# A two-layer hybrid trunk: rows summed on TensorE between the layers and at the end, packed query columns, and constant matmuls ahead of estimated waits

## The chip, the cores and the metric

The kernel runs on one core of a Trainium2 chip. Time is device time in microseconds (us) from start to end of one execution. A core has TensorE (PE in the profile; PEld is its weight load), VectorE (DVE), ScalarE (ACT), GpSimd (POOL) and SyncE (SP), which run their own instruction streams and wait for each other by semaphores; matmuls write to PSUM, here eight banks of 128x512 float32. TensorE's clock has two levels, 2.4 and 1.2 GHz; the profile shows the level that was granted (PEclk, 1.00 or 0.50).

## The reference

256 latent rows `x` and 256 context rows of 1024 channels go through two layers; only the 256 latent rows are the output. A layer is

```python
h = rms_norm(x, norm1_g) * (1.0 + sc1) + sh1            # and hc from the context rows
... = split_in(h @ w_in)                                # for Hyena, gated DeltaNet (GDN), latent attention (MLA)
q = (rms_norm(cq, mla_q_norm_g) @ mla_w_uq)             # 8 heads of 64 plain + 32 rotary columns
qr_l = rope_2d(qr_l, row, col)                          # rotates the 32 columns in four groups of 8
mix = merge_branches(gate_l, y_hy, y_gdn, y_mla, w_out)
x = x + gt1 * mix
h2 = rms_norm(x, norm2_g) * (1.0 + sc2) + sh2
x = x + gt2 * moe_ffn(h2, ...)                          # top 2 of 16 experts, weighted by the gate
```

and the end is `rms_norm(x, final_norm_g)`. Layer 0 carries the context rows too (512 rows in all); layer 1 updates the latent rows alone.

## The kernel before

All matmuls are float32 in effect. Weights and activations of the mixers are split into two rounded halves each, and `mm3` (line 420) multiplies three of the four pairs; some smaller products are plain float32 matmuls, each of which the chip runs as two instructions. SBUF is an arena of 47 pages of 128x1024 float32 (`Arena`, line 145); every buffer named `pg` in the profile is a page or half page of it. PSUM banks are handed out in the order in which they came back (`bank`, `unbank`, lines 391 and 395).

The order of the work is not written by hand throughout. `Plan` (line 227) keeps an estimated clock for each engine and for each buffer; every instruction passes through a `Lane` (line 197), which enters it in the plan and then issues it. Weighted products are *items* (`Item`, line 336: loads, preparation, matmuls, a step after them) in one list for each layer (`layer`, line 2331), and long chains of small steps (GDN, Hyena, attention, routing) are *streams*, generators from which `tick` and `fill` take a step wherever the plan sees time. So a change of one piece can move others. Since each instruction is issued by `Lane`, almost all rows of the profile show its line, L210; they are told apart by engine, tile and time.

Stages: layer 0's mixers run to about 881 us, its experts to 1165, the step between the layers to 1199, layer 1's mixers to 1776, its experts to 2046, the end to 2079.

The pieces that the change touches:

- **Query projection** (`uq_item`, line 1600). One item for each head: its 96 columns are loaded, `swap` (line 863) copies the 32 rotary columns, exchanged in groups of eight, into columns 96 to 128, and 18 matmuls (6 blocks of 128 rows, three pairs) give the head's queries and their exchanged copy. Then ScalarE copies the plain 64 rows out of PSUM, and VectorE forms the rotation as two products and a sum. `abkr_item` (line 838) does the same for the key's rotary columns.
- **Experts.** Layer 0 takes the 16 experts one after the other. Layer 1 (`moe_sets`, line 2208) has 12 sets of four slots of 32 tokens, each slot with its expert: up products, activation, down products; then ScalarE and VectorE copy a set's 128x1024 result out of two banks, and GpSimd scatters its rows to the DRAM buffer `yd`, two rows for each token.
- **The overflow test** (`overflow`, line 2492). Every engine loads the largest expert count and jumps over the handling (line 2497) if no expert has more tokens than fit.
- **The sum** (`load_y`, line 2286, and `combine`, line 2295). The rows are loaded back from `yd`; for each tile of 128 tokens ScalarE scales the first row by its gate, VectorE adds the second times its gate, GpSimd multiplies by `gt2`, VectorE adds to `x`, ScalarE sums the squares. Between the layers that is four tiles; at the end two tiles in half rows, followed by the final RMS norm, in which GpSimd multiplies by the final gain.
- **Between the layers** the new rows are normalised (`norm_rows`) and transposed on TensorE against the identity (`cst`), for layer 1's projection.

Of the kernel before, what the change touches and what calls it, by code (L numbers as in the profile page):

```python
# [42 lines left out]
def _constants():  # L43
# [27 lines left out]
    ra, rb = np.zeros((128, SEQ)), np.zeros((128, SEQ))  # L71
    ra[32:64], ra[64:96] = c32, s32
    rb[64:96], rb[96:128] = c32, s32
    cols["ropeA"], cols["ropeB"] = ra, rb
# [122 lines left out]
class Lane:  # L197


    def __init__(self, plan, eng, name):  # L200
        self._plan, self._eng, self._name = plan, eng, name

    def __getattr__(self, op):
        f = getattr(self._eng, op)
        if not callable(f):
            return f

        def call(*a, **k):
# [3 lines left out]
        return call  # L212

# [13 lines left out]
class Plan:  # L227
# [5 lines left out]
    def __init__(self):  # L233
# [4 lines left out]
        self.warm = 0.0  # L238
# [12 lines left out]
    def when(self, ap):  # L251
        return max(self.done.get(k, 0.0) for k in self.keys(ap))

# [108 lines left out]
LAG = (2, 1)  # L362


class Trunk:
# [209 lines left out]
    def setup(self):  # L575
# [7 lines left out]
        self.yd = [self.dr.tile([1024 >> l, D], F32, name=f"yd{l}") for l in range(L)]  # L583
        self.tokd = [self.dr.tile([512 * NE, 1], I32, name=f"tokd{l}") for l in range(L)]
# [253 lines left out]
    def abkr_item(self, l):  # L838
# [8 lines left out]
        def prep0(pg):  # L847
            self.swap(pg, 32, 64, 8)

        def post(b):  # L850
            ab, kr, t2 = self.M.get(), self.M.get(), self.M.get()
            nc.scalar.copy(ab.f()[0:16], b[0:16, :])
            ra = self.c("ropeA")
            nc.vector.tensor_tensor(kr.f()[64:96, :SEQ], b[32:64, :SEQ], ra[32:64], op=OP.mult)
            nc.vector.tensor_tensor(t2.f()[64:96, :SEQ], b[64:96, :SEQ], ra[64:96], op=OP.mult)
            nc.vector.tensor_tensor(kr.f()[64:96, :SEQ], kr.f()[64:96, :SEQ], t2.f()[64:96, :SEQ], op=OP.add)
# [4 lines left out]
        return self.win(l, 0, 512, post, "abkr", loader, prep0)  # L861

    def swap(self, pg, a, b, k):

        src = pg[:, :, a:a + 32].rearrange("p k (u s c) -> p k u s c", u=2, s=2)
        dst = pg[:, :, b:b + 32].rearrange("p k (u s c) -> p k u s c", u=2, s=2)
        for u in range(2):
            for s in range(2):
                self.nc.vector.tensor_copy(dst[:, :, u, s, :], src[:, :, u, 1 - s, :])
# [730 lines left out]
    def uq_item(self, l, h):  # L1600

        nc, M = self.nc, self.M
        nt = 512 if l < L - 1 else 256
# [998 lines left out]
```

## Time and profile before

| quantity | value |
|---|---|
| times of three runs | 2080.86, 2086.78, 2089.03 us |
| median | 2086.78 us |
| the profiled execution: its time, its span | 2080.96 us, 2079.3 us |
| mean granted TensorE clock over the span | 0.940 |
| TensorE, VectorE busy | 1850.6 us (89%), 1300.7 us (63%) |
| ScalarE, GpSimd busy | 873.3 us (42%), 318.5 us (15%) |
| read from HBM | 391.94 MB, 200 GB/s over the span |

The share of an engine is an average over stages with different limits. A row of a timeline gives the start of a run of like instructions, its length, and in brackets how long the engine was idle before it and which engine or DMA ended that idle time. A float32 matmul counts as two instructions, so "x8" is four matmuls; a matmul of rounded halves is one instruction.

### The profile page before, as it was taken

How to read it: one execution, taken by the hardware profiler on the slowest of the kernel's cores; microseconds unless marked ns; L12 is line 12 of the kernel's file. 1: busy time of each engine (PE TensorE's matmuls, PEld its weight loads, DVE VectorE, ACT ScalarE, POOL GpSimd, SP SyncE). 2: the span in 40 equal slices, each digit the busy share in tenths (PEclk: the TensorE clock that was granted, in tenths of full speed). 3: DMA queues.
4: the chain of work that ended last, by engine and by line, in shares of the span. 5: the costliest groups of instructions: out<-in, count | busy, mean ns of one | idle time of the engine just before them, and what ended most of it. 6: DMA issues, size and time to landing. Idle time of an engine off the chain costs nothing. (4 is left out here: it accounts for less than half of the span.)

```text
span 2079.3 us, 32681 instructions
## 1 busy us (share of the span) xinstructions
PE 1850.6 (89%) x12412; PEld 1369.9 (66%) x12413; DVE 1300.7 (63%) x2799; ACT 873.3 (42%) x1520; POOL 318.5 (15%) x314
## 2 busy tenths in 40 slices
PE   4899998899999989699999488998989977899993
PEld 1776786677768777588888366787768966233331
DVE  2667566654675669799999676777777755111113
ACT  3342423444434534288888444443455432111111
POOL 2212112000032204311110201131011310100002
PEclk8999999999999999799999798999989988999997
DMA  9717212412253274689998585622415529799961
GB/s 334 256 62 218 70 38 57 111 42 82 92 182 80 85 247 162 243 326 386 380 381 314 152 282 170 174 55 57 120 31 163 143 86 391 248 394 391 385 256 70
DMA packets 295184, 401.10 MB, mean 193 GB/s; under 512 B 43892, under 2 KB 185722, under 8 KB 295016
## 3 DMA queue, kind: packets, MB, share of 16 engines
q1 hardware_dynamic: 271512, 360.38, 51.5%
q0 software_dynamic: 13056, 27.15, 3.7%
q10 hardware_dynamic: 10448, 11.37, 1.7%
q8 instruction: 100, 1.64, 0.3%
q14 instruction: 68, 0.56, 0.1%
HBM read 391.94 MB, written 23.20 MB: 200 GB/s over the span
## 5 line engine op out<-in xcount | busy, mean ns | idle before, releaser
L210 PE MATMUL bank<-pg,pg 128*128 128x512 f32 (+6 forms) x10746 | 1659.6, 390 | 57.8 <-ACT pg L210 31.3
L210 PEld LDWEIGHTS bank<-pg,pg 128*128 128x128 f32 (+4 forms) x10746 | 1212.8, 167 | 455.9 <-issue 203.9
L210 DVE TENSOR_TENSOR pg<-pg,pg 128x1024 fp32r<-128x1024 f32 (+11 forms) x699 | 608.5, 903 | 157.7 <-ACT pg L210 147.8
L210 ACT CAST pg<-pg 128x1024 fp32r<-128x1024 f32 (+3 forms) x460 | 428.8, 965 | 209.7 <-DVE pg L210 139.0
L210 ACT COPY pg<-bank 64x256 f32<-64x256 f32 (+5 forms) x402 | 163.7, 440 | 285.1 <-PE bank L210 238.0
L210 PE MATMUL bank<-cst,pg 128*128 128x128 f32 (+3 forms) x935 | 142.5, 290 | 103.7 <-DVE pg L210 64.1
L210 PEld LDWEIGHTS bank<-cst,pg 128*128 128x128 f32 (+1 forms) x935 | 118.2, 159 | 147.4 <-issue 51.6
L210 POOL TENSOR_TENSOR pg<-pg,pg 128x512 f32<-128x512 f32 (+3 forms) x72 | 119.6, 1667 | 441.2 <-DVE pg L210 196.2
L210 ACT ACTIVATE pg<-bank 128x512 f32<-128x512 f32 (+1 forms) x116 | 61.0, 535 | 166.9 <-PE bank L210 156.3
L210 ACT ACTIVATE pg<-pg 128x512 f32<-128x512 f32 (+4 forms) x77 | 52.7, 692 | 146.8 <-DVE pg L210 107.1
L210 DVE SCALAR_TENSOR_TENSOR pg<-bank,vec,pg 128x510 f32<-128x510 f32 (+3 forms) x112 | 73.5, 657 | 54.6 <-ACT pg L210 52.8
L210 DVE SCALAR_TENSOR_TENSOR pg<-pg,bank 128x512 f32<-128x512 f32 (+1 forms) x92 | 54.2, 602 | 77.2 <-ACT pg L210 64.7
L210 POOL DMA_INDIRECT yd<-pg,t_vi x28 | 29.0, 1037 | 465.3 <-ACT pg L210 235.8
L210 DVE TENSOR_TENSOR pg<-bank,pg 128x512 fp32r<-128x512 f32 (+4 forms) x120 | 69.1, 596 | 27.3 <-ACT pg L210 14.6
L210 ACT CAST pg<-bank 128x512 fp32r<-128x512 f32 (+1 forms) x72 | 35.6, 517 | 100.4 <-PE bank L210 80.2
L210 DVE TENSOR_TENSOR pg<-pg,bank 128x512 f32<-128x512 f32 (+1 forms) x44 | 27.0, 613 | 80.6 <-PE bank L210 77.8
L210 POOL TENSOR_TENSOR pg<-pg 128x512 f32<-128x512 f32 (+1 forms) x12 | 14.3, 1193 | 400.0 <-ACT pg L210 348.3
L210 ACT ACTIVATE pg<-bank,t_amx,t_asq 128x512 f32<-128x512 f32 (+1 forms) x48 | 34.0, 708 | 77.4 <-DVE t_amx L210 77.4
L210 ACT ACTIVATE pg<-bank,vec 128x512 f32<-128x512 f32 (+3 forms) x64 | 41.4, 647 | 59.5 <-PE bank L210 53.6
L210 DVE COPY pg<-bank 128x512 f32<-128x512 f32 x12 | 8.3, 692 | 82.2 <-PE bank L210 75.3
L210 PE MATMUL bank<-pg,sc 128*32 128x512 f32 x384 | 53.5, 630 | 0.8 <-DMA pg<-in_w_ada_dram 0.7
L210 DVE TENSOR_REDUCE pg<-pg 128x128 f32<-128x1024 f32 (+15 forms) x128 | 43.1, 337 | 4.4
(258 smaller groups left out, 814.0 us busy)
## 6 DMA issues: line engine op xcount, KB each, us to landing
pg<-in_moe_w_dram SPq DMA_DIRECT2D x384, 512.0 KB
pg<-in_w_in_dram SPq DMA_DIRECT2D x120, 512.0 KB
pg<-in_w_ada_dram SPq DMA_DIRECT2D x96, 512.0 KB
pg<-in_w_out_dram SPq DMA_DIRECT2D x24, 512.0 KB
pg<-yd SPq DMA_DIRECT2D x12, 512.0 KB
pg<-in_mla_w_uq_dram SPq DMA_DIRECT2D x16, 288.0 KB
pg<-gcd POOLq DMA_DIRECT2D x16, 256.0 KB, 4.1
pg<-in_hy_out_dram SPq DMA_DIRECT2D x8, 512.0 KB
```

The costliest lines, as they stand in the source:

```text
L210: return f(*a, **k)
```

## The change

1. *Query projection.* Eight items become six: `rotary` items take the 32 rotary columns of four heads, `plain` items the 64 plain columns of two heads. The exchanged copy is no longer multiplied: VectorE makes it from the result with `stream_shuffle` by the index list `TURN`. `swap` is gone, and the constants of the rotation become two tables of 128 rows.
2. *Between the layers.* `combine` weights tiles 1 and 3 on TensorE: two diagonal matrices for a tile (`diagonals`, made before the rows are there) times the two rows, summed in PSUM. VectorE multiplies all tiles by `gt2`, GpSimd none.
3. *The end.* Layer 1's last two sets are not scattered. `tail_weights`, started at the first expert product of set 3, prepares each slot's gate (`gws`) and one-hot matrices from slots to tokens (`hot`); after set 9's scatter a stream `partial` adds what sets 0 to 9 left in `yd` (whose rows are zeroed early in the layer by `zero_rows`); and `finish` adds the last two sets by eight matmuls with `hot`, then normalises and stores. The handling of overflow zeroes the rows and adds them again.
4. *Constant matmuls.* Ahead of a transpose, or of a matmul that starts a sum, `keep_busy` asks the plan how long TensorE would wait. Between 1.5 and 14 us by that estimate, it fills 0.6 of it with matmuls of the identity by itself into the place that the next instruction overwrites. That gives 133 such matmuls in 14 places.

```diff
+        if self._name == "tensor" and (op == "transpose" or k.get("start")):
+            self.keep_busy(op, a, k)
...
+    def keep_busy(self, op, a, k):
+        plan, o = self._plan, a[0]
+        w = math.prod(o.shape[1:])
+        gap = plan.begin("tensor", op, a, k) - plan.clk["tensor"]
+        if plan.off or self._filling or plan.idle is None or o.shape[0] != 128 or w < 64 or not 1500 < gap < 14000:
+            return
+        w = min(w, 128)
+        c = 2 * max(4 + 0.84 * 128, 38 + 0.835 * w)
+        self._filling = True
+        for _ in range(int(0.6 * gap / c)):
+            self.matmul(o[:, :w], plan.idle, plan.idle[:, :w], start=True, stop=True)
+        self._filling = False
...
+DIAG = (1, 3)
+TAIL = (NSET - 2, NSET - 1)
+TURN = [i ^ 8 for i in range(32)]
...
+        def rotary(it):
+            r, t = M.get(), M.get()
+            nc.scalar.copy(r.f(nt), it.b[:, :nt])
+            self.unbank(it.b)
+            x, y = t.f(SEQ), t.f(SEQ, SEQ)
+            v.stream_shuffle(y, r.f(SEQ), TURN)
+            v.tensor_tensor(x, r.f(SEQ), self.c("ropeC"), op=OP.mult)
+            v.tensor_tensor(y, y, self.c("ropeS"), op=OP.mult)
+            for j in range(4):
+                q = self.qt[4 * i + j] = M.get()
+                p = slice(32 * j, 32 * j + 32)
+                v.tensor_tensor(q.f(SEQ)[64:96], x[p], y[p], op=OP.add)
...
+                if n in TAIL:
+                    for hf, b in enumerate(st.pop((n, "y"))):
+                        nc.vector.scalar_tensor_tensor(y.f(512, 512 * hf), b, self.gws[:, n - TAIL[0]:n - TAIL[0] + 1], self.gt2[0].f(512, 512 * hf), op0=OP.mult, op1=OP.mult)
+                        self.unbank(b)
+                    self.tail[n] = y
+                    return
...
+                if n == TAIL[0] - 1:
+                    self.start("partial", self.partial(l))
...
+    def add_rows(self, l, t, eng):
+        nc, v = self.nc, self.nc.vector
+        src = self.yd[l][256 * t:256 * t + 256].rearrange("(p k) d -> p k d", k=2)
+        y0, y1 = self.M.get(2), self.M.get(2)
+        for i, y in enumerate((y0, y1)):
+            eng.dma_start(out=y.f(), in_=src[:, i, :])
+        yield self.plan.when(y1.f())
...
+    def finish(self, l):
...
+        for hf in range(2):
+            for j, n in enumerate(TAIL):
+                for t in range(2):
+                    if j == 0:
+                        bank[t] = self.bank()
+                    nc.tensor.matmul(bank[t], self.hot.f(128, 128 * (2 * j + t)), self.tail[n].f(512, 512 * hf), start=j == 0, stop=j == len(TAIL) - 1)
+            for t in range(2):
+                x = self.xt[t].f(512, 512 * hf)
+                v.tensor_tensor(x, x, bank[t], op=OP.add)
...
-    def combine(self, tiles, ys, parts, after):
+    def combine(self, ys, after):
...
+        for t in DIAG:
+            for hf in range(2):
+                b = bank[t, hf] = self.bank()
+                for i in range(2):
+                    nc.tensor.matmul(b, self.dg[t].f(128, 128 * i), ys[t, i].f(512, 512 * hf), start=i == 0, stop=i == 1)
...
-        items += [self.ukv_item(l)] + [self.uq_item(l, h) for h in range(8)]
+        items += [self.ukv_item(l)] + [self.uq_item(l, kind, i) for kind, i in (("rotary", 0), ("plain", 0), ("plain", 1), ("rotary", 1), ("plain", 2), ("plain", 3))]
```

Three places in TensorE's order. In its rows `bank` is the place in PSUM that is written, behind `<-` stand its two inputs, `cst` is the constants' buffer with the identity, and the numbers behind `pg` are the page and its use. The first place is TensorE in layer 0, ahead of the transposes of GDN that start at 759.38 us. Before:

```order
L210 MATMUL bank_67<-pg_81_421,pg_514_5780 128x512 x2
L210 MATMUL bank_67<-pg_81_421,pg_515_5781 128x512
L210 MATMUL bank_67<-pg_82_430,pg_514_5780 128x512 x2
L210 MATMUL bank_67<-pg_82_430,pg_515_5781 128x512
L210 MATMUL bank_64<-cst_71,pg_492_5374 128x128 x2
L210 MATMUL bank_64<-cst_71,pg_447_4766 128x128 x2
L210 MATMUL bank_68<-cst_71,pg_492_5374 128x128 x2
L210 MATMUL bank_68<-cst_71,pg_447_4766 128x128 x2
```

After:

```order
L210 MATMUL bank_64<-pg_83_422,pg_491_5290 128x512 x2
L210 MATMUL bank_64<-pg_83_422,pg_492_5291 128x512
L210 MATMUL bank_64<-pg_84_431,pg_491_5290 128x512 x2
L210 MATMUL bank_64<-pg_84_431,pg_492_5291 128x512
L210 MATMUL bank_63<-cst_71 128x128 x14
L210 MATMUL bank_63<-cst_71,pg_444_4718 128x128 x4
L210 MATMUL bank_69<-cst_71,pg_444_4718 128x128 x4
L210 MATMUL bank_66<-pg_298_3061,pg_517_5740 128x512 x2
```

The products of another stream stand ahead of the transposes in both; 14 constant matmuls now stand between, in the bank that the first transposes write.

The second is TensorE between the layers, from the jump of the overflow test to layer 1's first transposes. Before:

```order
L2511 UNCONDITIONAL_BRANCH x2
L2508 REGISTER_ALU
L2508 COMPARE_AND_BRANCH
L2508 UNCONDITIONAL_BRANCH
L2497 UNCONDITIONAL_BRANCH
L210 MATMUL bank_65<-cst_71,pg_1373_10008 128x128
L210 MATMUL bank_65<-cst_71,pg_1374_10010 128x128
L210 MATMUL bank_65<-cst_71,pg_1375_10012 128x128
L210 MATMUL bank_65<-cst_71,pg_1376_10014 128x128
```

After:

```order
L2628 UNCONDITIONAL_BRANCH
L2615 UNCONDITIONAL_BRANCH
L210 MATMUL bank_67<-pg_1343_9892,pg_1270_9538 128x512
L210 MATMUL bank_67<-pg_1344_9894,pg_1270_9538 128x512
L210 MATMUL bank_70<-pg_1343_9892,pg_1270_9538 128x512
L210 MATMUL bank_70<-pg_1344_9894,pg_1270_9538 128x512
L210 MATMUL bank_65<-pg_1347_9900,pg_1270_9538 128x512
L210 MATMUL bank_65<-pg_1348_9902,pg_1270_9538 128x512
L210 MATMUL bank_64<-pg_1347_9900,pg_1270_9538 128x512
L210 MATMUL bank_64<-pg_1348_9902,pg_1270_9538 128x512
L210 MATMUL bank_69<-cst_71 128x128 x21
L210 MATMUL bank_69<-cst_71,pg_1375_10005 128x128
```

Eight products with the diagonals and 21 constant matmuls now stand ahead of the first transpose.

The third is the end of TensorE's program. Before:

```order
L210 MATMUL bank_64<-pg_2100_17528,pg_2096_17507 128x512
L210 MATMUL bank_70<-pg_2100_17528,pg_2096_17507 128x512
L2511 UNCONDITIONAL_BRANCH x2
L2508 REGISTER_ALU
L2508 COMPARE_AND_BRANCH
L2508 UNCONDITIONAL_BRANCH
L2497 UNCONDITIONAL_BRANCH
```

After:

```order
L2628 COMPARE_AND_BRANCH
L2628 UNCONDITIONAL_BRANCH
L2615 UNCONDITIONAL_BRANCH x2
L210 MATMUL bank_68<-pg_2057_17283,pg_1870_15563 128x512
L210 MATMUL bank_66<-pg_2057_17283,pg_1870_15563 128x512
L210 MATMUL bank_68<-pg_2058_17318,pg_1870_15563 128x512
L210 MATMUL bank_66<-pg_2058_17318,pg_1870_15563 128x512
L210 MATMUL bank_70<-pg_2057_17283,pg_1870_15563 128x512
L210 MATMUL bank_69<-pg_2057_17283,pg_1870_15563 128x512
L210 MATMUL bank_70<-pg_2058_17318,pg_1870_15563 128x512
L210 MATMUL bank_69<-pg_2058_17318,pg_1870_15563 128x512
```

Where the program ended with the jump, eight matmuls with the one-hot page now follow; for each half the first of the two sets goes into both banks, then the second.

## Rows read from the trace of the kernel before

**Rows 1.** First part of the page: busy time, share, instructions of each engine.
```profile
PE 1850.6 (89%) x12412; PEld 1369.9 (66%) x12413; DVE 1300.7 (63%) x2799; ACT 873.3 (42%) x1520; POOL 318.5 (15%) x314
```

**Rows 2.** Timeline, end of the span: start, duration, engine, operation, [idle before, releaser].
```profile
2033.49 12.22 PE L210 MATMUL bank<-pg,pg 128*32 128x512 f32 x112
...
2045.79 0.69 DVE L210 COPY pg<-bank 128x512 f32<-128x512 f32 x1 [6.17 <-PE bank L210]
...
2068.68 2.22 DVE L210 TENSOR_SCALAR t_fss<-t_fss 128x2 f32<-128x2 f32 x1
...
2072.95 1.15 ACT L210 ACTIVATE pg<-pg,t_finb 128x1024 f32<-128x1024 f32 x1 [4.50 <-DVE t_finb L210]
...
2074.13 0.34 ACTq L210 DMA_DIRECT2D out_dram<-pg  x1
```

**Rows 3.** Timeline between the layers.
```profile
1177.37 1.28 DVE L210 SCALAR_TENSOR_TENSOR pg<-pg,t_gw,pg 128x1024 f32<-128x1024 f32 x1 [14.50 <-DMA pg<-yd]
...
1179.30 1.15 ACT L210 ACTIVATE pg<-pg,t_gw 128x1024 f32<-128x1024 f32 x1 [2.07 <-DMA pg<-yd]
...
1183.23 3.38 DVE L210 SCALAR_TENSOR_TENSOR pg<-pg,t_gw,pg 128x1024 f32<-128x1024 f32 x1
...
1198.85 1.04 PE L210 MATMUL bank<-cst,pg 128*128 128x128 f32 x3 [33.45 <-DVE pg L210]
```

**Rows 4.** Timeline of TensorE at three waits.
```profile
319.17 1.22 PE L210 MATMUL bank<-pg,pg 128*128 128x512 f32 x2 [7.02 <-ACT pg L210]
...
759.38 2.15 PE L210 MATMUL bank<-cst,pg 128*128 128x128 f32 x8 [4.86 <-DVE pg L210]
...
1702.06 1.11 PE L210 MATMUL bank<-cst,pg 128*128 128x128 f32 x4 [7.07 <-DVE pg L210]
```

**Rows 5.** Windows: us, busy of each engine (instructions), PEclk, DMA share, GB/s.
```profile
319.20:324.50 5.30, 4.92 (x11) 3.43 (x12) 5.09 (x12) 0.87 (x1) 2.00 (x2) 0.50 0.01 3
759.40:764.90 5.50, 5.50 (x17) 4.41 (x18) 3.33 (x5) 1.98 (x3) 0.00 (x0) 0.50 0.87 299
```

**Rows 6.** Timeline of TensorE; group by line and form: busy, mean ns.
```profile
36.10 1.98 PE L210 MATMUL bank<-pg,pg 64*128 64x512 f32 x4
...
48.93 3.78 PE L210 MATMUL bank<-pg,pg 64*128 64x512 f32 x4
...
L210 PE MATMUL bank<-pg,pg 128*128 128x128 f32 x724 | 100.0, 294 | 5.8 <-DVE pg L210 4.5 <-ACT pg L210 1.0
```

**Rows 7.** Timeline, set 9's scatter; DMA issues: count, KB each, us to landing.
```profile
2019.04 0.98 POOL L210 DMA_INDIRECT yd<-pg,t_vi  x1 [21.48 <-DVE pg L210]
...
pg<-xd POOLq DMA_DIRECT2D x2, 512.0 KB, 8.1
...
yd<-pg,t_vi POOLq DMA_INDIRECT x28, 6.9
```

**Rows 8.** Timeline of ScalarE's copies of query items; matmuls by form.
```profile
402.33 0.58 ACT L210 COPY pg<-bank 64x512 f32<-64x512 f32 x1
...
412.94 0.58 ACT L210 COPY pg<-bank 64x512 f32<-64x512 f32 x1
...
1425.09 0.37 ACT L210 COPY pg<-bank 64x256 f32<-64x256 f32 x1 [1.17 <-PE bank L210]
...
1459.32 0.37 ACT L210 COPY pg<-bank 64x256 f32<-64x256 f32 x1 [0.23 <-PE bank L210]
...
L210 PE MATMUL bank<-pg,pg 128*128 128x256 f32 x1872 | 253.0, 294 | 10.6 <-ACT pg L210 5.6 <-DVE pg L210 4.9
```

**Rows 9.** Line 2497, overflow test: min/median/max ns, first to last start us.
```profile
L2497 SPq EVENT_SEMAPHORE  x18: 17/17/17, 1136.6 to 2010.6; - x18
...
L2497 DVEq EVENT_SEMAPHORE  x4: 21/21/21, 1162.9 to 2046.8; - x4
...
L2497 SPq COMPARE_BRANCH  x2: 50/52/53, 1131.5 to 2004.3; - x2
L2497 DVEq COMPARE_BRANCH  x2: 63/68/72, 1162.3 to 2046.2; - x2
```

More of the change, by code (lines that the diff above doesn't have):

```diff
@@ L237, in __init__ @@
         self.cur, self.sin, self.off = None, False, False
-        self.warm = 0.0
+        self.warm, self.idle = 0.0, None
     @staticmethod
@@ L860, in post @@
             self.start("gates", self.gdn_gates(l, ab))
[L861 to L869, printed above, removed]
+        return self.win(l, 0, 512, post, "abkr", loader)
     def gdn_gates(self, l, ab):
@@ L1622, in mm @@
                 x.free()
-            if h == 7:
+            if kind == "plain" and i == 3:
                 for hi, lo in self.lora["q"]["x"]:
@@ new lines, in combine @@
+        ss, s8 = self.tiny(4, "css"), self.tiny(8, "css8")
+        bank = {}
+        for t in DIAG:
+            for hf in range(2):
+                b = bank[t, hf] = self.bank()
+                for i in range(2):
+                    nc.tensor.matmul(b, self.dg[t].f(128, 128 * i), ys[t, i].f(512, 512 * hf), start=i == 0, stop=i == 1)
+            self.dg[t].free()
+        for t in range(4):
+            g, x = self.gt2[t // 2], self.xt[t]
+            y0, y1 = ys[t, 0], ys[t, 1]
+            if t in DIAG:
+                for hf in range(2):
+                    o = 512 * hf
+                    v.tensor_tensor(y0.f(512, o), bank[t, hf], g.f(512, o), op=OP.mult)
+                    self.unbank(bank[t, hf])
+                    v.tensor_tensor(x.f(512, o), x.f(512, o), y0.f(512, o), op=OP.add)
+                    nc.scalar.activation(y1.f(512, o), x.f(512, o), AF.Square, accum_out=s8[:, 2 * t + hf:2 * t + hf + 1])
+            else:
+                nc.scalar.activation(y0.f(), y0.f(), AF.Copy, scale=self.gw[0][:, t:t + 1])
+                v.scalar_tensor_tensor(y0.f(), y1.f(), self.gw[1][:, t:t + 1], y0.f(), op0=OP.mult, op1=OP.add)
+                v.tensor_tensor(y0.f(), y0.f(), g.f(), op=OP.mult)
+                v.tensor_tensor(x.f(), x.f(), y0.f(), op=OP.add)
+                nc.scalar.activation(y1.f(), x.f(), AF.Square, accum_out=ss[:, t:t + 1])
+            y0.free()
+            y1.free()
+            after(t)
@@ L2331, in layer @@
+        for t in DIAG:
+            v.tensor_tensor(ss[:, t:t + 1], s8[:, 2 * t:2 * t + 1], s8[:, 2 * t + 1:2 * t + 2], op=OP.add)
+        return ss
     def layer(self, l):
@@ L2351, in layer @@
         items = [self.abkr_item(l)] + ([hook(self.late_setup)] if l == 0 else []) + qkv(0)
+        items += [hook(lambda: self.zero_rows(l, nc.gpsimd))] if l == L - 1 else []
         items += [self.dft_item(l)] + [self.z_item(l, h) for h in (0, 1)]
@@ L2453, in build @@
             else:
[L2454 to L2467 removed]
+                self.finish(l)
             for g in self.gt2:
@@ L2497, in overflow @@
         with tc.If(most > CAP[l]):
+            if l == L - 1:
+                self.zero_rows(l, nc.sync)
             blk = self.M.get()
@@ L2512, in overflow @@
                         self.overflow_part(l, e, j)
+            if l == L - 1:
+                for t in range(2):
+                    for _ in self.add_rows(l, t, nc.sync):
+                        pass
         self.plan.off = False
```

168 lines of the change are left out of this document (95 added, 73 removed).

## The prediction

> **What bounds the kernel now.** I read the page's first part first: TensorE is busy for 1850.6 of 2079.3 us, and no other engine passes 63% [rows 1]. So most of the span is TensorE's own work, and a matmul taken out of a saturated stretch is worth its whole duration. Then I looked for stretches in which TensorE does nothing. Two are long. One stands at the end: the last matmul ends 33.6 us before the span does [rows 2]. The other lies between the layers: TensorE starts at 1198.85 after 33.45 us without work [rows 3]. The remaining waits are short, but after them the granted clock stands at its lower level, 1.2 instead of 2.4 GHz, for some microseconds of full work [rows 4, 5]. The change touches all of these, so I price it by place, against the profiled execution of 2080.96 us (span 2079.3 us). That execution lies at the lower end of the runs shown; their median is 2086.78.
>
> **Part 1, the end.** Before, the last matmul ends at 2033.49 + 12.22 = 2045.71 and the span ends 33.6 us later, at 2079.3 [rows 1, 2]. In between lie the copies out of PSUM, a scatter to DRAM, the load back, the weighted sum of 256 rows, the RMS norm and the store. After, the last two sets never go to DRAM. Their product is weighted on VectorE, multiplied by one-hot matrices and added to a stream that already holds sets 0 to 9. I rebuild the chain from 2045.71:
> - The second half is weighted as long as the copy there takes, 0.69 us, until 2046.5; the first half is done about 0.9 us earlier, since its matmuls end first. The first one-hot matmul writes the bank that this first half frees (the order rows show the same bank number), so it starts at about 2046.1.
> - Eight float32 matmuls of 512 columns: two such (four instructions, since float32 runs as two) took 1.98 us at the full clock, so 0.99 each, 7.9 us, until 2054.0. At the lower clock two took 3.78, so 1.89 each [rows 6]; TensorE has been working until 2045.71, so I take the full clock.
> - The last addition takes 0.7 us (as the copy of a half row) and the product with the final gain about 1.3, until 2056.0; the squares on ScalarE run beside it.
> - The norm's small steps: from 2068.68 to 2072.95 they took 4.27 us, of which one, run beside GpSimd's product, took 2.22 [rows 2]. GpSimd does nothing here after the change, so I take 2.4 us, until 2058.4.
> - The scaling, 1.15 us on ScalarE as before and about 1.3 on VectorE, until 2059.7; then the store, 2079.3 - 2074.13 = 5.2 us [rows 2], until 2064.9.
>
> That is 14.4 us less. What hides the rest: the sum over sets 0 to 9 moves ahead of the last two sets' end. Set 9's scatter is issued at 2019.04; a scatter lands in 6.9 us in the median and a 512 KB load from GpSimd's queue takes up to 8.1 [rows 7], so four loads issued behind it land by about 2038, and two rounds of ScalarE and VectorE (about 4 us each) end by 2046. VectorE does them before it weights sets 10 and 11, so this cover is thin: it is behind by as much as the loads are late. The loads wait on GpSimd's queue, behind which nothing else is queued then. The ends for this part are 17 (norm steps and adds closer than I laid them) and 8 us. I take 14.
>
> **Part 2, the query projection.** Eight items of 18 matmuls per layer become six, since four heads' rotary columns now fill one item and the swapped copy of them is no longer multiplied but shuffled on VectorE. In layer 0 TensorE sets the pace there: the items' copies follow each other from 402.33 to 412.94 in three steps, 3.54 us each [rows 8]. Two items less: 7.1 us. In layer 1 the copies go from 1425.09 to 1459.32 in seven steps, 4.9 us each, with other work in between; the matmuls alone cost 18 x 253.0/1872 = 2.4 us an item [rows 8]. So between 4.9 and 9.8 us for two; I take 5, nearest to the matmuls' own time. The swaps on VectorE go too, and what replaces them is shorter; I price this at nothing, since the items' pace has it already. The new loads come in shorter runs; they are issued ahead of their use, so nothing again, and up to 2 us if that lead is gone.
>
> **Part 3, between the layers.** Before, four tiles go through ScalarE, VectorE, GpSimd and VectorE. One multiply-add on VectorE took 3.38 us there, beside GpSimd's product, as against 1.28 alone [rows 3]. After, GpSimd is out of it; tiles 0 and 2 cost VectorE three passes of about 1.25 us each, tiles 1 and 3 four of 0.69 each, 13 us in all from 1177.4 on, so 1190.5 if nothing waits. But tile 1 waits for four float32 matmuls which can start only when its rows are there (1179.30 for the first, by ScalarE's wait on the same kind of load), and TensorE has then been idle for 14 us: at 1.89 each two of them end at 1183.1 and four at 1186.9. Tile 2's scaling stands behind tile 1's squares on ScalarE, in order. This pushes the last square to about 1197, about 1 us later than before, with ends of 4 more and 3 less (if the clock rises within the first four).
>
> **Part 4, the filler.** At 14 places, 133 matmuls of 128 columns by constants stand ahead of a matmul of which the planner thinks that it waits. One such float32 instruction costs 100.0/724 = 0.138 us and so a matmul 0.276 [rows 6]; 21 of them stand in the idle stretch between the layers, the other 112 are 31 us of work. Where the wait is real they cost nothing. The three largest places have real waits: 7.02 us at 319.17 (13 fillers, 3.6 us), 4.86 at 759.38 (14, 3.9 us), 7.07 at 1702.06 (15, 4.1 us) [rows 4]. What they can give back is the lower clock behind these waits: behind the first two TensorE is busy for 4.92 and 5.50 us at 1.2 GHz [rows 5], half of which is 5.2 us, and with the third of the same kind about 7.8. But 3.4, 1.0 and 3.0 us of each wait stay idle, and the rows do not tell whether the clock holds through that. I take half, 4 us; the ends are a gain of 13 (five places that give 2.6 each) and a loss of 4 (fillers ahead of work that was ready).
>
> **The sum.** -14 - 7.1 - 5 + 1 - 4 = -29 us: 2052 on the scale of the profiled execution, 2058 on that of the median. I take the middle, **2055 us**.
>
> **The rivals.**
> - *The clock holds at every filled place.* Then part 4 gives 13 instead of 4: 2046 us. For it: three of the waits are as long as the estimate needs. Against: up to half of each stays idle.
> - *The branch ahead of the final sum is no longer covered.* The kernel tests for overflow between the last set and the sum, and jumps over the handling. Before, the scatter hides this. SyncE went from its branch at 1131.5 to its next instruction at 1136.6, 5.1 us, and from 2004.3 to 2010.6 at the latest, 6.3; VectorE needed 0.6 (2046.2 to 2046.8) [rows 9]. If TensorE or VectorE pays what SyncE did, the end keeps 8 instead of 14 us: 2061. Against it: VectorE's own row. The Trainium skill, Runtime: NRT & Kernel Launch, section Instruction fetch mechanics, has a rule for this: a taken branch to a target outside the small window already fetched waits for the fetch of it. By that rule the end would lose these 5 to 6 us; SyncE's rows agree with it, VectorE's don't.
> - *The weights don't come earlier.* The last stage, from 1776 on, reads its weights while TensorE works without a pause. If that stream, not TensorE, set the stage's end, all that is won ahead of it (15 us) would be lost and only the end's 14 remain: 2070. Against it: the loads wait for pages that the work ahead frees, so they move with it.
> - *The filler stands in front of ready work.* If the schedule that comes out has its waits elsewhere, the 112 fillers are 31 us on the path, and twice that at the lower clock: 2059 + 31 to 62 = 2090 to 2121 us, slower than before. It decides once more than 30 us of them lie on the path. Against it: the three largest places match real waits.
> - *The change does not do what it says*: the fillers leave the clock as it is and cost nothing. 2059 us, within the forecast's own range.
>
> **How the numbers follow.** The forecast, with its own range of 2046 to 2063, has 0.60; the clock that holds 0.14; the branch 0.10; the weights 0.09; the filler on the path 0.04; 0.03 is left for moved work that I have not priced. The range has to take in the clock's case and the weights': 2040 to 2071. About 0.5% (10 us) is what a measurement of this kernel can tell from no change. Faster by more than that, below 2076: 0.93. Within it: 0.04, the milder half of the filler case. Slower: 0.03.
>
> **What would show it.** In the profile after: the end of the last set's matmuls to the end of the span near 19 us instead of 33.6, with eight matmuls of about 1 us in it and no DMA but the store; six query items per layer, at the same pace; the wait ahead of layer 1's first transposes replaced by eight matmuls at the lower clock and 21 fillers; the granted clock at 2.4 GHz just after 319 and 759 us. It is wrong if the last stretch stays above 26 us, if the last stage of matmuls grows, or if matmuls of constants are seen while the work behind them had nothing to wait for.

## The result and the profile after

The changed kernel takes 2055.8 us (median of four runs, 2054.2 to 2058.84) against 2087.23 of the kernel before: ratio 0.9857, 95% interval 0.9833 to 0.9880. The forecast was 2055. The profiled execution spans 2054.4 us, 24.9 less than the one before; the medians lie 31.4 apart, since the profiled execution of before was one of its shortest.

The page's first part of the kernel after, to be held against [rows 1]:

```profile
PE 1880.6 (92%) x12638; PEld 1395.7 (68%) x12639; DVE 1279.6 (62%) x2732; ACT 869.6 (42%) x1520; POOL 304.5 (15%) x320
```

TensorE is busy for 30 us more in a span that is 25 us shorter. 32.8 us of its work are constant matmuls (266 instructions, 133 matmuls), and the products of the two new sums take 7.1 us at the end and 9.9 between the layers; the packed queries take off less than these add.

The same transposes and products of TensorE in both traces tell where the time went. First the timeline of before, then that of after (start, length, operation, [idle ahead, releaser]): the transposes that follow the query items of layer 0, those ahead of its experts, and those ahead of the experts of layer 1; of after also the eight products with the diagonals, which are new between the layers.

```profile
434.93 1.03 PE L210 MATMUL bank<-cst,pg 128*128 128x128 f32 x8
...
881.19 1.11 PE L210 MATMUL bank<-cst,pg 128*128 128x128 f32 x4 [5.67 <-DMA pg<-h2d,t_gi]
...
1776.17 1.12 PE L210 MATMUL bank<-cst,pg 128*128 128x128 f32 x4 [6.63 <-DMA pg<-h2d,t_gi]
```

```profile
319.21 1.22 PE L210 MATMUL bank<-pg,pg 128*128 128x512 f32 x2 [4.12 <-ACT pg L210]
...
418.89 1.04 PE L210 MATMUL bank<-cst,pg 128*128 128x128 f32 x8
...
868.72 1.54 PE L210 MATMUL bank<-cst,pg 128*128 128x128 f32 x6 [6.10 <-DMA pg<-h2d,t_gi]
...
1169.05 9.94 PE L210 MATMUL bank<-pg,pg 128*128 128x512 f32 x16 [14.92 <-DMA pg<-yd]
...
1189.39 0.87 PE L210 MATMUL bank<-cst,pg 128*128 128x128 f32 x2 [5.71 <-DVE pg L210]
...
1767.39 1.97 PE L210 MATMUL bank<-cst,pg 128*128 128x128 f32 x8 [6.72 <-DMA pg<-h2d,t_gi]
...
2024.14 12.22 PE L210 MATMUL bank<-pg,pg 128*32 128x512 f32 x112
```

With [rows 2 to 4] that gives, start by start:

| up to | before | after | so far | this stretch |
|---|---|---|---|---|
| the wait of 7.02 us in [rows 4] | 319.17 | 319.21 | 0.0 | 0.0 |
| end of layer 0's query items | 434.93 | 418.89 | -16.0 | -16.0 |
| layer 0's experts | 881.19 | 868.72 | -12.5 | +3.6 |
| layer 1's first transposes | 1198.85 | 1189.39 | -9.5 | +3.0 |
| layer 1's experts | 1776.17 | 1767.39 | -8.8 | +0.7 |
| last expert products, start | 2033.49 | 2024.14 | -9.4 | -0.6 |
| end of the span | 2079.3 | 2054.4 | -24.9 | -15.6 |

So in this trace nearly all of it comes from two places, the query items of layer 0 and the end; some 7 us are given back in between. Layer 1's packed queries show no gain here: from its first transposes to its experts it takes 0.7 us more than before. The experiments below say why. The end, timeline of after, to be held against [rows 2]:

```profile
2009.68 0.98 POOL L210 DMA_INDIRECT yd<-pg,t_vi  x1 [21.48 <-DVE pg L210]
...
2017.11 1.15 ACT L210 ACTIVATE pg<-pg,t_gw 128x1024 f32<-128x1024 f32 x1 [1.40 <-DMA pg<-yd]
...
2027.61 2.48 DVE L210 TENSOR_TENSOR pg<-pg,pg 128x1024 f32<-128x1024 f32 x2
...
2035.58 1.61 DVE L210 SCALAR_TENSOR_TENSOR pg<-bank,t_gws,pg 128x512 f32<-128x512 f32 x2 [4.16 <-PE bank L210]
...
2036.84 7.10 PE L210 MATMUL bank<-pg,pg 128*128 128x512 f32 x16 [0.48 <-PEq L2615]
...
2045.99 0.17 DVE L210 TENSOR_SCALAR t_fss<-t_fss 128x2 f32<-128x2 f32 x1
...
2048.22 1.15 ACT L210 ACTIVATE pg<-pg,t_finb 128x1024 f32<-128x1024 f32 x1 [2.79 <-DVE t_finb L210]
```

The last expert product ends at 2024.14 + 12.22 = 2036.36, and 18.0 us are left instead of 33.6. The sum over sets 0 to 9 is done at 2030.1, six microseconds ahead of that, so its cover is not thin. TensorE waits 0.48 us for its own sequencer at the jump of the overflow test (L2615), eight one-hot matmuls take 7.1, and the small steps run at 0.2 us each.

### The profile page after: what moved, and what is told of

Read it like the earlier page. It is cut to its first block, busy times and chain, and to the rows that moved or that the text cites. A ratio compares the mean times of both kernels' runs of the same rounds, so it can differ in the third digit from the quotient of the medians.

```text
span 2054.4 us, 33092 instructions
## 1 busy us (share of the span) xinstructions
PE 1880.6 (92%) x12638; PEld 1395.7 (68%) x12639; DVE 1279.6 (62%) x2732; ACT 869.6 (42%) x1520; POOL 304.5 (15%) x320
## 5 line engine op out<-in xcount | busy, mean ns | idle before, releaser
L210 PE MATMUL bank<-pg,pg 128*128 128x512 f32 (+7 forms) x10704 | 1661.0, 391 | 52.1 <-DVE pg L210 19.7
L210 PEld LDWEIGHTS bank<-pg,pg 128*128 128x128 f32 (+5 forms) x10704 | 1208.8, 167 | 452.9 <-issue 222.1
L210 DVE TENSOR_TENSOR pg<-pg,pg 128x1024 fp32r<-128x1024 f32 (+13 forms) x687 | 600.3, 906 | 150.9 <-ACT pg L210 142.1
L210 ACT CAST pg<-pg 128x1024 fp32r<-128x1024 f32 (+2 forms) x456 | 424.3, 966 | 185.0 <-DVE pg L210 125.5
L210 ACT COPY pg<-bank 64x256 f32<-64x256 f32 (+4 forms) x398 | 162.5, 441 | 293.4 <-PE bank L210 262.7
L210 POOL TENSOR_TENSOR pg<-pg,pg 128x512 f32<-128x512 f32 (+3 forms) x64 | 100.4, 1572 | 429.6 <-DVE pg L210 197.9
```

## The experiments

Twelve kernels, each timed against the kernel before on the same chip. Times are medians in us.

| run | what it is | us | ratio | 95% interval |
|---|---|---|---|---|
| p_uq | before + queries | 2058.59 | 0.9873 | 0.9849 to 0.9897 |
| p_end | before + end | 2068.51 | 0.9923 | 0.9894 to 0.9952 |
| p_comb | before + diagonals | 2087.74 | 1.0009 | 0.9992 to 1.0026 |
| p_fill | before + constant matmuls | 2085.10 | 1.0003 | 0.9990 to 1.0016 |
| x_noswap | before, copies left out | 2079.19 | 0.9959 | 0.9943 to 0.9976 |
| a_uqend | queries + end only | 2047.52 | 0.9821 | 0.9795 to 0.9847 |
| a_nofill | after, no constant matmuls | 2050.72 | 0.9835 | 0.9808 to 0.9861 |
| a_oldcomb | after, old sum between layers | 2042.66 | 0.9804 | 0.9774 to 0.9834 |
| a_keep | after, stores moved | 2050.29 | 0.9840 | 0.9819 to 0.9861 |
| p_ghost | before + unplanned matmuls | 2085.41 | 1.0000 | 0.9985 to 1.0015 |
| p_ghost9 | the same, more of them | 2083.19 | 1.0000 | 0.9986 to 1.0014 |
| c_fill9 | a_oldcomb, more of them | 2042.41 | 0.9796 | 0.9775 to 0.9816 |

### The four parts, each alone on the kernel before

**p_uq**

```diff
-        items += [self.ukv_item(l)] + [self.uq_item(l, h) for h in range(8)]
+        items += [self.ukv_item(l)] + [self.uq_item(l, kind, i) for kind, i in (("rotary", 0), ("plain", 0), ...
```

> The kernel before plus the six query items and the key's rotation by shuffle alone. The profile after shows layer 0's stretch from 325 to 435 us shorter by 17 to 19 us, where the prediction priced 7.1 for the matmuls. Theory A1 (VectorE's copies of rotary columns held the items up, so the gain belongs to this part alone): that stretch is shorter by 15 to 19 us, its VectorE time falls by about 10 us, and the kernel takes about 2070 us. Theory A2 (the prediction's: the matmuls alone): shorter by 7 to 8 us, about 2075 us in all with layer 1. Theory B (the gain of 19 needs the filler at 388 us): 10 to 12 us.

Measured: 26 us less (21 to 31), more than any of the theories gave it, and without the other parts. Its profiled execution is the slowest of the four (2065.63 us); there, the way from the wait at 320 us to layer 0's experts is 9.2 us shorter than before (552.83 for 562.02) with 10.0 us less work on VectorE (356.67 for 366.71). The same window and that of layer 1's mixers, from its first transposes to its experts (columns as in [rows 5]):

```profile
320.46:873.29 552.83, 512.93 (x3034) 403.21 (x3034) 356.67 (x835) 224.24 (x436) 97.39 (x87) 0.95 0.41 128
1193.61:1761.13 567.52, 493.32 (x3954) 426.55 (x3954) 391.22 (x1035) 244.92 (x496) 82.79 (x95) 0.92 0.50 156
```

Layer 1's mixers took 577.3 us before (1776.17 - 1198.85), so they are 9.8 us shorter. The transposes behind layer 0's query items come 9.1 us earlier after the wait, not 15 to 19, but there the planned order differs: 24 more instructions of other products stand ahead of them than before. **p_end**:

```diff
+TAIL = (NSET - 2, NSET - 1)
...
+                self.finish(l)
```

> The kernel before plus the new end alone (last two sets not scattered, one-hot matmuls, sum over sets 0 to 9 earlier). Theory A: from the last expert matmul to the end of the span 18 us instead of 33.6, as after, and 2071 to 2073 us in all. Rival: the zeroing of the rows early in layer 1 and the gate preparation at set 3 cost something ahead of the end, up to 5 us, which the whole change hides elsewhere: 2076 us with the same 18 us at the end.

Measured: 16 us less, as the 15.6 at the end of the trace after; from the last expert product to the end it takes 18.6 us in its trace, and the rival's cost ahead of the end doesn't show. **p_comb**:

```diff
-                ss = self.combine(range(4), ys, 1, keep)
+                ss = self.combine(ys, keep)
```

> The kernel before plus the weighting by diagonals between the layers alone. The profile after has 35.3 us between the last expert matmul of layer 0 and layer 1's first transpose, against 33.45 before. Theory A: the stretch is 34 to 37 us here too and the kernel takes 2087 to 2091 us (predicted: 1 us more than before). Rival: taking GpSimd out makes it shorter, 30 to 32 us, and the lengthening seen after belongs to the 21 constant matmuls ahead of the transposes: 2084 us.

Measured: no difference that can be told from none, with the lean to the side of slower. The stretch from layer 0's last expert product to the first transpose is 34.1 us in its trace, as the first theory had it. **p_fill**:

```diff
+            if self._name == "tensor" and (op == "transpose" or k.get("start")):
+                self.keep_busy(op, a, k)
...
+        self.plan.idle = self.c("ident")
```

> The kernel before plus the constant matmuls alone. Theory A (the parts act one by one and their gains add; the prediction gave the filler 4 us, with ends of 13 gained and 4 lost): about 2083 us against 2087 of the kernel before; no stretch of TensorE work is later by over 2 us; the lower-clock time behind the filled places falls, at 319 us from 10.2 to about 7 us. Theory B (a part that is put in alone also shifts the planned order, and the shift is as large as the part): between 2080 and 2095, with the change far from the filled places.

Measured: nothing, within some 3 us to either side. In its trace layer 1's mixers take 582.8 us instead of 577.3, more than the 2 us that the first theory allowed for any stretch. By the ratios the four parts alone sum to 26.5 + 16.1 - 1.9 - 0.6 = 40 us, where the whole change gives 30.

### What is missing in the sum

**a_nofill**:

```diff
-        self.plan.idle = self.c("ident")
```

> The changed kernel without its constant matmuls. Alone they moved nothing on the kernel before (ratio 1.0003), while the query part alone gave 26 us and the end alone 16, 42 together, where the whole change gives 30. Theory C (the constant matmuls cost what is missing once the queries are packed, since some of them then stand ahead of work that is ready): 2043 to 2048 us. Theory D (they are neutral here too, the gains of the queries and of the end are not additive): 2054 to 2059 us.

**a_uqend**:

```diff
-        self.plan.idle = self.c("ident")
...
-                ss = self.combine(ys, keep)
+                ss = self.combine(range(4), ys, 1, keep)
```

> The kernel before with the packed queries and the new end only: old sum between the layers, no constant matmuls. If the two parts add: 2042 to 2047 us. If each alone gained partly from the same place (its shift changed what was late in layer 1), 2053 to 2058 us, and the stretch of layer 1 before its expert sets is longer here than with the queries alone.

Queries and end together give 37 us, so these two add, within the interval. Without constant matmuls the changed kernel comes out between the two theories, and the interval overlaps that of the whole change. **a_oldcomb** keeps the constant matmuls and takes the diagonals out:

```diff
-                self.diagonals()
...
-                ss = self.combine(ys, keep)
+                ss = self.combine(range(4), ys, 1, keep)
```

> The changed kernel with the old sum between the layers (no diagonals; queries, end and constant matmuls as changed). Theory: the diagonals cost 1 to 3 us as they did alone (ratio 1.0009), so 2052 to 2055 us, with 33 to 34 us between the last expert matmul of layer 0 and the first transpose instead of 35.3. Rival (they cost the missing 10 us, by what they delay behind the first transposes): 2044 to 2048 us.

Measured: 2042.66, just below the rival's range; its interval touches that of the changed kernel (0.9834 and 0.9833). Where do the diagonals cost? Not between the layers: from layer 0's last expert product to the first transpose it is 35.3 us with them (1189.39 - 1169.05 + 14.92) and 35.4 without. It comes later, in layer 1's mixers. Windows of them, of before, of a_oldcomb, and of the kernel after:

```profile
1198.85:1776.17 577.32, 501.49 (x3989) 433.31 (x3990) 402.81 (x1079) 245.67 (x495) 86.47 (x95) 0.92 0.50 155
```

```profile
1183.93:1750.51 566.58, 501.66 (x4064) 435.04 (x4064) 390.95 (x1035) 245.31 (x496) 87.34 (x100) 0.94 0.51 160
```

```profile
1189.39:1767.39 578.00, 508.04 (x4073) 439.91 (x4074) 392.08 (x1035) 244.96 (x496) 86.37 (x100) 0.93 0.50 156
```

The 10 us that the packed queries win there (567.5 in p_uq, 567.6 in a_uqend, 566.6 here) are gone in the kernel after; in a_nofill, with diagonals but without constant matmuls, half of them is (572.8). The whole times say the same: by the ratios' midpoints the diagonals cost 3 us without constant matmuls (a_uqend, a_nofill) and 11 with them (a_oldcomb, the change), though the first two intervals overlap and the other two touch. So, as far as midpoints and single traces tell, what is missing in the sum is mostly the price of the diagonals beside packed queries and constant matmuls, which p_comb, without either, couldn't show. One cause is seen. After the diagonals, an engine of layer 1's start waits for a store; the timeline of the kernel after:

```profile
1205.82 0.97 SPq L210 DMA_DIRECT2D xd<-pg  x2
...
1214.56 1.05 ACT L210 CAST pg<-pg 128x1024 fp32r<-128x1024 f32 x1 [3.85 <-DMA xd<-pg]
...
1243.05 0.80 PE L210 MATMUL bank<-pg,pg 128*128 128x256 f32 x2 [2.41 <-ACT pg L210]
```

and of a_oldcomb, the same products of TensorE:

```profile
1183.93 1.04 PE L210 MATMUL bank<-cst,pg 128*128 128x128 f32 x3 [35.38 <-DVE pg L210]
...
1234.40 0.51 PE L210 MATMUL bank<-pg,pg 128*128 128x256 f32 x2 [0.51 <-ACT pg L210]
```

SyncE issues the stores of the finished latent rows (`xd`) behind its queue of weight loads, some 30 us after the rows are there (GpSimd, below, can issue them at once), and until they are out their pages are read. With the diagonals the page that ScalarE writes next is one of these. a_nofill has the same wait (4.54 us on ScalarE), p_comb too (4.34 on VectorE), though its layer 1's mixers are no longer for it than before's (576.3 us); before, a_uqend and a_oldcomb have none. **a_keep** takes the cause away:

```diff
-                        nc.sync.dma_start(out=self.xd[128 * t:128 * t + 128], in_=self.xt[t].f())
+                        nc.gpsimd.dma_start(out=self.xd[128 * t:128 * t + 128], in_=self.xt[t].f())
```

> The changed kernel with the two stores of the finished latent rows to DRAM between the layers issued by GpSimd's queue instead of SyncE's. In all three kernels with diagonals an engine of layer 1's start waits 3.9 to 4.5 us for that store, since it writes a page that the store still reads; in the three kernels without them none does. Theory S (the diagonals' cost is this wait, and what follows it): the wait at 1214 us is gone, layer 1's first gates come 3 to 4 us earlier against the first transposes, and the kernel takes 2050 to 2053 us instead of 2055.8. Rival (the wait only moves to the next late page, or the price lies in the planned order of layer 1's attention): 2054 to 2058 us.

The timeline of a_keep:

```profile
1165.21 0.61 POOL L210 DMA_DIRECT2D xd<-pg  x1 [8.45 <-DVE pg L210]
...
1183.19 1.14 PE L210 MATMUL bank<-cst,pg 128*128 128x128 f32 x3 [5.35 <-DVE pg L210]
...
1233.57 0.50 PE L210 MATMUL bank<-pg,pg 128*128 128x256 f32 x2 [0.58 <-ACT pg L210]
```

From the first transpose to these products it is 50.4 us, as in a_oldcomb (50.5), instead of 53.7: so this wait is the price at this place, and it is gone. Layer 1's mixers take 570.4 us in this trace. The whole kernel lies at 0.9840, inside the range expected, but its interval overlaps that of the changed kernel, so in the total the gain is not shown. What remains between a_keep and a_oldcomb (570.4 and 566.6 in layer 1's mixers) is not settled; the planned order of layer 1's attention differs between the two.

### Why the query items gave so much

**x_noswap**:

```diff
+            nc.sync.dma_start(out=blk.f(768).rearrange("p (k c) -> p k c", k=6)[:, :, 96:128], in_=w[:, :, 96 * h + 64:96 * h + 96])
...
-            self.swap(p.f(768).rearrange("p (k c) -> p k c", k=6), 64, 96, 6)
```

> The kernel before with its eight query items as they are, but the rotary columns' copy in columns 96 to 128 is loaded a second time instead of exchanged by VectorE, so that the rotation takes the wrong partner: the four copies of VectorE for each item are left out, every matmul stays. Theory A1 (VectorE's copies held the items up): layer 0's stretch from 325 to 435 us is shorter by 8 to 12 us and the kernel takes 2067 to 2075 us. Theory A2 (the matmuls of the two dropped items made all of the gain): the stretch keeps its length within 2 us, 2083 to 2087 us.

Measured: 8.6 us less by the ratio (5 to 12), 2079.19 us, between the two theories: the copies held the work up, but they are about a third of the part's 26. In the kernel before, the chain that TensorE waits for is seen at 387.63: VectorE's four copies, ScalarE's rounding of the item behind them, then the first product.

```profile
386.25 0.47 DVE L210 COPY pg<-pg 128x48 f32<-128x48 f32 x4
...
386.75 0.83 ACT L210 CAST pg<-pg 128x768 fp32r<-128x768 f32 x1 [0.57 <-DVE pg L210]
...
387.63 0.74 PE L210 MATMUL bank<-pg,pg 128*128 128x512 f32 x2 [3.47 <-ACT pg L210]
```

In the trace of x_noswap TensorE doesn't wait there; its products follow the transposes ahead of them, at 387.09. Up to layer 0's experts nothing of that is left in this trace, of its slowest execution (563.7 us from the wait at 320 us, for 562.0 before), and layer 1's mixers are 3.8 us shorter (573.5). So the copies' price is shown for the whole time, and not place by place.

Windows from the wait at 319 us to the transposes behind layer 0's query items, of before, and of after. TensorE's work in them is the same but for the two items (36 instructions), one product more, and 20 instructions of constant matmuls:

```profile
319.17:434.93 115.76, 107.12 (x661) 85.95 (x661) 73.35 (x181) 44.94 (x83) 8.06 (x10) 0.95 0.30 80
```

```profile
319.21:418.89 99.68, 97.89 (x644) 80.72 (x645) 63.66 (x138) 44.63 (x83) 9.98 (x10) 0.95 0.39 93
```

That is 16.1 us less: TensorE is busy for 9.2 us less, of which two items are 7.1 at the pace of [rows 8], and idle for 1.8 us instead of 8.6; VectorE has 9.7 us less to do.

### Why the constant matmuls gave nothing on the kernel before

**p_ghost** and **p_ghost9** issue them past the plan, so that all else keeps the order of the kernel before. Against p_fill:

```diff
-            self.matmul(o[:, :w], plan.idle, plan.idle[:, :w], start=True, stop=True)
+            self._eng.matmul(o[:, :w], plan.idle, plan.idle[:, :w], start=True, stop=True)
...
-        ... not 1500 < gap < 14000:
+        ... not 1500 < gap < 40000:
-        for _ in range(int(0.6 * gap / c)):
+        for _ in range(int(0.9 * gap / c)):
```

(The last four lines are p_ghost9 alone.)

> The kernel before with 109 constant matmuls in 13 places that the plan doesn't know of: all other matmuls keep their order, where the plan's knowledge of them reordered layer 1's attention. Theory F1 (constant matmuls hold the clock up; entered in the plan they lose it again by the new order): 2078 to 2082 us against 2086, TensorE's lower-clock time smaller by 25 us or more. Theory F2 (they give nothing, whatever the order): 2084 to 2088 us.

> As the run before, with 0.9 of each estimated wait filled instead of 0.6, and the wait between the layers too (93 matmuls there, 26 us of 33 at the full clock). Theory F1: another 2 to 4 us less than with 0.6, no lower clock behind the filled places except where the wait was longer than estimated; 2075 to 2080 us. Theory F2: 2084 us or more, since some of the 260 now stand ahead of work that is ready.

The mean granted clock goes from 0.940 to 0.947 and 0.957, and the time stays: ratio 1.0000 both times, within 0.15%; p_ghost9's 2083.19 us lies between its two theories. Two mechanisms show in p_ghost (L213 and L230 are the helper's lines there). The first, in the timeline of TensorE behind 380 us and in a window:

```profile
379.97 3.07 PE L230 MATMUL bank<-cst 128*128 128x128 f32 x26
385.23 0.73 PE L213 MATMUL bank<-pg,pg 128*128 128x512 f32 x2 [2.19 <-ACT pg L213]
386.29 3.96 PE L213 MATMUL bank<-pg,pg 128*128 128x512 f32 x16 [0.33 <-DVE pg L213]
391.74 0.73 PE L213 MATMUL bank<-pg,pg 128*128 128x512 f32 x2 [1.48 <-ACT pg L213]
392.73 39.96 PE L213 MATMUL bank<-pg,pg 128*128 128x512 f32 x170 [0.26 <-DVE pg L213]
```

```profile
387.00:390.40 3.40, 3.26 (x15) 2.30 (x13) 2.02 (x5) 1.24 (x2) 0.00 (x0) 1.00 0.00 0
```

The kernel before, the same work and the same length of window:

```profile
388.70 6.18 PE L210 MATMUL bank<-pg,pg 128*128 128x512 f32 x18 [0.32 <-DVE pg L210]
395.13 39.96 PE L210 MATMUL bank<-pg,pg 128*128 128x512 f32 x170 [0.26 <-DVE pg L210]
```

```profile
389.40:392.80 3.40, 3.40 (x10) 2.61 (x9) 2.03 (x5) 1.23 (x2) 0.00 (x0) 0.50 0.00 0
```

Before, the products behind the wait run at half the clock, 6.18 us for 18; with the constant matmuls at the full clock, 3.96 for 16. But the next item isn't ready earlier, TensorE waits 1.48 us for ScalarE, and the long row of products starts 7.50 us behind the wait both times (395.13 - 387.63, 392.73 - 385.23). The second: a constant matmul writes the place that is written next, and where the wait is for that place, it waits too and then runs ahead of the real work.

```profile
1514.40 3.39 PE L230 MATMUL bank<-cst 128*128 128x128 f32 x16 [3.04 <-DVE pg L213]
1517.55 1.66 PE L213 MATMUL bank<-pg,pg 128*128 128x256 f32 x12
```

Here 3.2 us are added to a wait that the kernel before has too (its products there start at 1509.80 after 3.26 us). In the kernel after no constant matmul waits so. **c_fill9** asks whether more of them pay on the faster variant, a_oldcomb:

```diff
-        ... not 1500 < gap < 14000:
+        ... not 1500 < gap < 40000:
-        for _ in range(int(0.6 * gap / c)):
+        for _ in range(int(0.9 * gap / c)):
```

> The changed kernel with the old sum between the layers (2042.7 us, ratio 0.9804) and with 0.9 instead of 0.6 of each estimated wait filled, the long one between the layers too. Theory F2, by which constant matmuls are worth nothing on this kernel since the time won behind a wait is waited again at the next value from VectorE or ScalarE: 2040 to 2047 us, though the granted clock's mean rises. Theory F1 (more of them is better once the waits are real): 2034 to 2039 us.

They don't: 0.9796 against 0.9804, at a mean granted clock of 0.963 instead of 0.955. This interval (up to 0.9816) lies clear of the changed kernel's (from 0.9833): queries, end, the old sum and constant matmuls are faster than the change as made. Whether the first helping of them pays there is open: a_oldcomb's four runs (2039.08 to 2046.1 us) all lie below a_uqend's (2047.0 to 2050.97), which has none and was timed against the same runs of the kernel before, but the two intervals overlap. In the traces layer 0's experts start at 864.4 and 866.9 us with queries and constant matmuls (a_oldcomb, c_fill9), at 873.3, 872.3 and 872.1 with queries alone (p_uq, a_uqend, a_nofill). What p_ghost shows holds for the kernel before.

## Why the prediction was right, step by step

The time came out as forecast, 2055.8 for 2055, but not by the sum as written, and that it fits so well is luck. One term, the queries', was less than half of what it should be, 12 us for 26; and the diagonals and the filler, 3 us of gain together in the forecast, cost some 7 by the ratios' midpoints (0.9821 without either, 0.9857 with both; the intervals overlap). The two errors nearly cancel.

- **The end**, 14 us: right, 15.6 in the trace, 16 alone. The last expert product to the end of the span takes 18.0 us where the chain gave 19.2; the one-hot products 7.1 instead of 7.9, the small steps 2.2 instead of 2.4, as laid out without GpSimd beside them. The cover was called thin and is not: the first rows were back 7.4 us after set 9's scatter was issued (2009.68 to 2017.11), where I allowed 19 for all of them, and the second tile's didn't wait. The first one-hot product starts 0.48 us behind the last expert product, as the chain had it (0.4), but by the profile it waits for TensorE's own sequencer and not for a bank; the order rows that the chain refers to for the bank don't show the last expert products of the kernel after.
- **The query items**, 7.1 + 5: mis-sized, 26 us alone. The failed step is "I price this at nothing, since the items' pace has it already", on VectorE's swaps. The pace of 3.54 us per item was read from three steps in which TensorE is full; the items ahead of it waited for the chain of copy, rounding and difference. Leaving the copies out is worth 8.6 us alone. The products left out are the 12 us forecast by their own time; the rest, some 6 us, lies inside the intervals of the two ratios, or in the shorter chain of two items less, which no run separates. By place, p_uq's trace has 9.2 us ahead of layer 0's experts and 9.8 in layer 1's mixers, where 7.1 and 5 were priced. In the trace after it is 12.5 up to layer 0's experts, and nothing in layer 1.
- **Between the layers**, +1: right for the place (34.1 us in p_comb for 33.45; the 35.3 of the kernel after are no more than the 35.4 of a_oldcomb, which has no diagonals), wrong for the cost. The step looked no further than layer 1's first transposes. What the new order did to the pages, and with them to a store that was late all along, cost 3.3 us just behind, and layer 1's mixers as a whole take 578.0 us with diagonals and constant matmuls where a_oldcomb takes 566.6.
- **The filler**, -4: wrong on the kernel before, 0 within some 3 us. Beside the other parts its worth isn't shown: by midpoints it gains 4 us without the diagonals (0.9804 for 0.9821) and loses 5 with them (0.9857 for 0.9835), with overlapping intervals. Two things failed. The clock rose only in part: windows of the kernel after, at the two places of [rows 5], show 0.50 again behind 319 us, where 4.12 us of the wait stayed idle, and 0.69 behind the other.

```profile
319.20:324.50 5.30, 4.91 (x11) 3.42 (x12) 5.09 (x13) 0.90 (x1) 2.03 (x2) 0.50 0.00 0
746.80:752.30 5.50, 5.34 (x19) 3.89 (x20) 3.29 (x5) 2.18 (x3) 0.00 (x0) 0.69 0.39 135
```

And where it rose, as behind 385 us in p_ghost, the step that prices it at half the lower-clock work is wrong: the engine that caused the wait sets the pace of the next products too.

The rivals: *the clock holds* came true for the clock in part, and for the time not at all. *The branch* costs TensorE 0.48 us at the end, 1.85 in a_nofill, not 5 to 6; VectorE needs 0.7 (2036.8 to 2037.5). TensorE's queue takes the branch while the last products still run: its row starts 2.3 us ahead of their end and lasts 1.24 us here, 3.64 in a_nofill, where it ends behind them. By the Trainium skill (Runtime: NRT & Kernel Launch, Instruction fetch mechanics) a taken branch to a target outside the window already fetched waits for the fetch of the target. Rows of such different length fit that, but no run shows what they wait for. The rows of the overflow test at the end (min/median/max ns, first to last start), of the kernel after, and of a_nofill:

```profile
L2615 DVEq EVENT_SEMAPHORE  x2: 21/21/21, 2037.4 to 2037.5; - x2
L2615 PEldq COMPARE_BRANCH  x1: 1237/1237/1237, 2034.0 to 2034.0; - x1
L2615 DVEq COMPARE_BRANCH  x1: 56/56/56, 2036.8 to 2036.8; - x1
```

```profile
L2614 PEldq COMPARE_BRANCH  x1: 3636/3636/3636, 2031.1 to 2031.1; - x1
```

*The weights don't come earlier* fell: the expert stage of layer 1 keeps its lead to within 0.6 us. *The filler in front of ready work* didn't decide: at four of the 14 places of the kernel after no wait is left behind the constant matmuls (1.3 us of them at 59 us, 2.4 at 388, 1.1 at 1542, 1.6 at 1750), 6.4 us in all, and at the first two the kernel before waits 1.41 and 3.47 us; it takes over 30. *The change does not do what it says* came out half: the clock did rise (0.940 to 0.947 in p_ghost), but on the kernel before that is worth nothing, as this rival priced it.

## What to carry to other kernels

Before an engine's idle time or lower clock is priced, ask what ends the *next* wait: here a faster TensorE behind a wait on ScalarE only waited longer at the next value. Small preparatory steps on VectorE that look free by its busy share can set the pace of a TensorE-bound stage if they stand in the chain from load to product. And when a step between two stages is reordered, look at the late stores of the stage before: they hold pages, and whoever is given one of them pays. Two parts that cost nothing alone, as the diagonals and the constant matmuls here, can cost something together, so test them in the whole too.

The version to keep is the one with the queries and the end alone and the old sum between the layers: 2042 to 2048 us in the three kernels built so, with or without constant matmuls. Of the three only c_fill9 is clear of the change as made by its interval.

## What the runs showed of the hardware

The same instructions in the same order do not take the same time from execution to execution, by some microseconds. The kernel after and a_oldcomb issue the same work on TensorE up to the end of layer 0's experts; at 728 us they are level, and by the experts of layer 0 one is 5.6 us behind. Timeline of the kernel after, and a window of it:

```profile
733.98 6.45 PE L210 MATMUL bank<-pg,pg 128*128 128x128 f32 x28 [3.43 <-DVE pg L210]
...
883.32 1.14 PE L210 MATMUL bank<-cst,pg 128*128 128x128 f32 x9
```

```profile
734.50:737.90 3.40, 3.40 (x12) 2.92 (x12) 0.20 (x1) 0.90 (x3) 0.53 (x1) 0.50 0.89 290
```

and of a_oldcomb:

```profile
732.48 4.95 PE L210 MATMUL bank<-pg,pg 128*128 128x128 f32 x28 [2.14 <-DVE pg L210]
...
877.74 0.71 PE L210 MATMUL bank<-cst,pg 128*128 128x128 f32 x5
```

```profile
733.00:736.40 3.40, 3.40 (x23) 3.04 (x23) 0.53 (x2) 0.90 (x3) 1.06 (x2) 1.00 0.83 295
```

A wait of 3.43 us was followed by the lower clock, one of 2.14 us was not; why VectorE was later in the one isn't seen. So 5.6 of the 17 us between these two profiled executions are no effect of the diagonals, and a difference of a few microseconds between two single traces, far from the place of an edit, says nothing. The kernel before ran from 2078.27 to 2089.78 us in 19 runs beside the four parts.
